# Two exponentials of a softmax head taken apart, and other places for the first loads of the tail

## Chip, cores and metric

One core of one Trainium2 chip. The metric is the device time of one execution in microseconds, median of several runs. Engines: TensorE (PE) with its weight loads (PEld), VectorE (DVE), ScalarE (ACT), GpSimd (POOL), and SyncE (SP), which only starts DMAs here. Each engine works through its own program in order; semaphores hold an instruction until what it reads, or what stands in the buffer that it writes, is done.

## The reference

One layer of a trunk with 1024 latent tokens, 128 context tokens and 256 cached ones, D_MODEL 1024, all float32:

```python
h = _rmsnorm(x, norm_g) * (1 + scale) + shift
u, v, g_a, c_q, c_kv, k_rope, g_b = _split_in(h @ w_in)
a_out = _chunk_mlp(u, v, w_s, b_s, g_v) * jax.nn.silu(g_a)
q = (_rmsnorm(c_q, q_norm_g) @ w_uq).reshape(B, L, MLA_HEADS, QK_NOPE + QK_ROPE)
...
s = jnp.concatenate(logits, axis=-1).astype(jnp.float32) * ATTN_SCALE
p = jax.nn.softmax(s, axis=-1).astype(v_all.dtype)
return jnp.einsum('bhqk,bkhv->bqhv', p, v_all)
...
y = jnp.concatenate([a_out, attn * jax.nn.silu(g_b)], axis=-1) @ w_o
return x + gate * y
```

Four heads attend from each block of 128 latent tokens to 1280 keys (1024 latent, 256 cached). The outputs of both halves go through w_o (1024 x 1024), are added to x under the gate, and get a last RMS norm.

## The kernel before

Precision is kept by splitting float32 values in two: a high part, which is a cast on ScalarE or POOL, and a low part, which DVE subtracts (lo_of, L112); a product is then three matmuls (high by high, high by low, low by high).

Up to 317 us the kernel normalises, projects and prepares queries and keys; the change leaves that alone. **Attention** follows, to about 505 us. There are 8 blocks t of 128 queries and 4 heads h; the head (t, h) is a step, two heads a pair. A period of PE's program holds the scores of one pair (score_steps, L1515 to L1519: one matmul group of 256 cached keys, two of 512 latent keys, for each head) and, merged between them by cost, the value stream of an earlier pair: five groups i = 0 to 4 of four 128x128 transposes (tr, L1562) into a PSUM ring of two buffers, and behind each the weighted sums with the compressed values (av, L1586 to L1588), then the copy os of the sums (L1596, ACT), their product with wuv (L1605) and the multiplication into mixB (L1607, DVE).

What sets the order on the other engines is `later(dt, fn)` (L167): the step is put into the program when PE's planned time has gone dt microseconds past the call. So the numbers in those calls fix the row in which an operation stands on ACT, DVE and POOL; at run time nothing overtakes.

softmax() (L1464 to L1510) plans for each head: the maximum over latent scores (L1481) and cached ones (L1484) and the shift nb (L1486 and L1487, or L1489) on DVE; exps (L1495), two ScalarE instructions, first 256 columns, then 1024, into e; divide: sum and reciprocal rs (L1499, L1500, DVE) and the multiplication of all 1280 columns (L1501, POOL). For each transposed group ACT casts the high part ph (L1566) and DVE subtracts the low part pl (L112); the subtraction frees the PSUM buffer for the group after next.

Beside the attention of blocks 1 to 5 run the units: weight sums T1 to T4 of quarters of w_o (t_unit, L1874), two a head pair, with subtractions on POOL (L809), casts thi on ACT (L1885), low parts into traw on DVE (L112), and stores to tdram by SP (L1881). From block 6 on pieces of w_o are split instead (spare_hi on POOL L115, spare_lo on DVE L112; the tiles area, ringB, ringC, kch, krh).

From 505 to 531 us the last two pairs' value streams run with early output products. The **output projection** (531 to 608 us) is a product by blocks with fewer multiplications; its left blocks (ring areas, made from mixA and mixB by casts L2152 and copies L2150 with lo_of) meet the sums T1 to T4 from tdram (t_pieces, L1919, DMAs issued by POOL; three matmuls at L1923 to L1925). A list planner (Plan, L45) orders its steps by cost, priority and due time; fetch (L2046) plans its loads one behind the other. The buffers of its pool ep lie over those of the attention pool, so a load can start only when the last reader of what lay there is done: `t1` (all of T1) lay over four tiles, two of them pieces of w_o, gate0 (loaded at L2053 by SP, read first at L2197) over the exponentials of head (7, 1) and the high part of the last transposed group.

Of the kernel before, what the change touches and what calls it, by code (L numbers as in the profile page):

```python
# [9 lines left out]
F32 = mybir.dt.float32  # L10
F32R = mybir.dt.float32r
BF16 = mybir.dt.bfloat16
I32 = mybir.dt.int32
AF = mybir.ActivationFunctionType
ALU = mybir.AluOpType
# [3 lines left out]
P = 128  # L19
NT = 9  # L20
NS = 8
# [73 lines left out]
def tile_hymba_step(ctx: ExitStack, tc: tile.TileContext, I, O):  # L95
    nc = tc.nc
    V, S, G, T = nc.vector, nc.scalar, nc.gpsimd, nc.tensor

    def opened(name, bufs=1, space=None, side=None):
        kw = dict(name=name, bufs=bufs, reuse_waits="tile")  # L100
        if space is not None:
            kw["space"] = space
        if side is not None:
            kw["side"] = side
        cm = tc.tile_pool(**kw)
        return cm, cm.__enter__()
# [60 lines left out]
    def later(dt, fn):  # L167
        waiting.append((now[0] + dt, fn))
        waiting.sort(key=lambda w: w[0])
# [17 lines left out]
    def step(cost, fn):  # L187

        catch_up(now[0])
        for f in list(fill):  # L190
            if f[0] in made and made_at[f[0]] <= now[0]:
                fill.remove(f)
                run(f[1:])
        run((cost, fn))
# [58 lines left out]
    tdram = gd.tile([4, P, 4, 2, 512], F32R, tag="tdram", name="tdram")  # L253
    scl = pc.tile([P, NT], F32, tag="scl", name="scl")
# [541 lines left out]
    def sums(n, k):  # L796
        c = 3072 * n + 768 * k
        return wide(c, GW), wide(c + GW, GW)

    T2, T3 = ([sums(n, k) for k in range(4)] for n in range(2))  # L800
    T4 = {k: sums(2, k) for k in range(2)}
    T1 = [(hh[k, 1], hl[k, 1]) for k in range(4)]
    t1 = {}
# [594 lines left out]
    if True:  # L1398
# [24 lines left out]
        c_kv, kv = opened("kv", side="left")  # L1423
# [4 lines left out]
        vh = kv.tile([P, 11, P], F32R, tag="vh", name="vh")  # L1428
        vl = kv.tile([P, 11, P], F32R, tag="vl", name="vl")
# [37 lines left out]
    units, traw, unit_of, paced = [], {}, [], [0]  # L1467
# [3 lines left out]
    def softmax(t, h, lat_, con_):  # L1471

        m = sm.tile([P, 2], F32, tag="m", name=f"m{t}{h}", bufs=3)
        nb = sm.tile([P, 1], F32, tag="nb", name=f"nb{t}{h}", bufs=3)
        su = sm.tile([P, 2], F32, tag="su", name=f"su{t}{h}", bufs=3)
        rs = sm.tile([P, 1], F32, tag="rs", name=f"rs{t}{h}", bufs=3)
        e = ap_.tile([P, 1280], F32, tag="e", name=f"e{t}{h}", bufs=6)
        es[t, h] = e

        def start():  # L1480
            V.tensor_reduce(m[:, 0:1], lat_, axis=AX.X, op=ALU.max)  # L1481

        def shift():
            V.tensor_reduce(m[:, 1:2], con_, axis=AX.X, op=ALU.max)  # L1484
            if units or t < 2 or (t, h) == (NS - 1, 3):
                V.tensor_reduce(nb, m, axis=AX.X, op=ALU.max)  # L1486
                V.tensor_scalar(nb, nb, nscl[:, t : t + 1], None, op0=ALU.mult)  # L1487
            else:
                V.scalar_tensor_tensor(nb, m[:, 0:1], m[:, 1:2], nscl[:, t : t + 1], op0=ALU.max, op1=ALU.mult)  # L1489
            later(0.6, exps)  # L1490
            later(1.3, lambda: spare_lo(1))

        def exps():
            for i, (src, sl) in enumerate(((con_, slice(1024, 1280)), (lat_, slice(0, 1024)))):
                S.activation(e[:, sl], src, AF.Exp, bias=nb, scale=scl[:, t : t + 1], accum_out=su[:, i : i + 1])  # L1495
            later(2.5 if t == 0 or (t, h) < (1, 2) else 1.9, divide)

        def divide():
            V.tensor_tensor(rs, su[:, 0:1], su[:, 1:2], op=ALU.add)  # L1499
            V.reciprocal(rs, rs)  # L1500
            G.tensor_scalar(e, e, rs, 0.0, op0=ALU.mult, op1=ALU.add)  # L1501
            made.add(("e", t, h))
            spare_hi(1 if his and his[0] in heavy else 2)
            spare_lo(2)
            if units and units[0][0] in traw:
                n_ = 1
                paced[0] += 1
                for i in range(n_):
                    unit_of[0](*units.pop(0), 2.2 * i)

        return start, shift
# [121 lines left out]
    def spare_hi(n):  # L1633
        for _ in range(min(n, len(his))):
            his.pop(0)()

    def spare_lo(n):
        for _ in range(min(n, len(los))):
            los.pop(0)()
# [148 lines left out]
    with tc.manual_schedule(engines=engines):  # L1788
# [77 lines left out]
        th, tl, his_ = {}, {}, {}  # L1866
# [46 lines left out]
        def t_pieces(m, k, hold, wide=512):  # L1913

            rows = hold.rearrange("p (a c) -> p a c", c=wide)[:, :, wide - 512 :]
            n = rows.shape[1] // 2
            for i in range(n):
                th[m, k + i], tl[m, k + i] = rows[:, 2 * i], rows[:, 2 * i + 1]
            G.dma_start(rows, tdram[m - 1, :, k : k + n].rearrange("p k s c -> p (k s) c"))  # L1919
# [37 lines left out]
        first = [s_ for i in range(LEAD) for s_ in score_steps(*heads[i])]  # L1957
# [61 lines left out]
    c_ep, ep = opened("ep", side="right")  # L2019
# [2 lines left out]
    spare_hi(len(his))  # L2022
    while los:
        spare_lo(1)
    t1 = ep.tile([P, 4096], F32R, tag="t1", name="t1")
    t4 = [ep.tile([P, 2048], F32R, tag="t4", name="t4"), *(kv.tile([P, 1024], F32R, tag=n, name=f"{n}t") for n in ("vh", "vl"))]
    fg = ep.tile([P, 1024], F32, tag="fg", name="fg")
    gate, ssq = {}, {}
    plan = Plan()
    plan.free.update(T=0.0, V=0.5, S=0.5, G=0.0, D=0.0)  # L2030
# [15 lines left out]
    def fetch(key, fn, deps=(), cost=1.35, lag=1.8):  # L2046
        last_ = [fetched[0]] if fetched[0] else []
        step(key, "D", cost, fn, [*deps, *last_], 0, lag=lag)
        fetched[0] = "|" + key

    def load_gate():
        gate[0] = ep.tile([P, 1024], F32, name="gate0", tag="gate0")
        nc.sync.dma_start(gate[0], gdram[0:1, :].broadcast_to([P, 1024]))  # L2053

    own = {}
# [1 line left out]
    def load_own(i, dma):  # L2057
        t_ = own[i] = ep.tile([P, 1024], F32, tag="xr", name=f"own{i}", bufs=4)
        dma(t_[:, 0:512], gdram[1:2, 512 * i : 512 * i + 512].broadcast_to([P, 512]))
        dma(t_[:, 512:1024], I["x"][8][:, 512 * i : 512 * i + 512])  # L2060

    fetch("gate0", load_gate, lag=4.5)
    for k in (0, 2):
        fetch(f"T1{k}", lambda k=k: t_pieces(1, k, t1[:, 1024 * k : 1024 * k + 2048]), cost=2.7)
    for k, piece in ((0, t4[0]), (2, t4[1]), (3, t4[2])):
        fetch(f"T4{k}", lambda k=k, piece=piece: t_pieces(4, k, piece), cost=1.35 if k else 2.7)
    fetch("own1", lambda: load_own(1, nc.scalar.dma_start))
    for t in (0, 1):
        fetch(f"x{t}", lambda t=t: load_xr(t))
# [71 lines left out]
    for q in range(3, len(queue)):  # L2141
        n, name, _ = queue[q]
# [96 lines left out]
            for t in PAIRS[nx]:  # L2239
                fetch(f"x{t}", lambda t=t: load_xr(t), {2: [], 3: ["a81"]}.get(t, [f"y{t - 4}"]))  # L2240

    landed = dict(T1=("T10", "T12"), T4=("T40", "T42", "T43"))

    def products():
        for q in range(1, 28):
# [174 lines left out]
```

## Time and profile before

| what | us |
|---|---|
| median of 3 runs | 617.89 (617.23 to 619.18) |
| the profiled execution | 617.24 |
| its span, first to last instruction | 615.5 |
| PE busy | 599.4 |
| DVE busy | 425.4 |
| ACT busy | 328.9 |
| POOL busy | 207.4 |
| mean granted clock of TensorE | 0.993 |

Busy time is that of one profiled execution. A row of the timeline gives start, duration, engine, line, operation, the tile written and those read, shapes, and in brackets how long the engine had been idle before it and which instruction's end it waited for. Where a helper records the operation (L112, L115, L809), the tile names tell which use it is. Ends of matmuls are modelled; starts are measured. Numbers of heads and blocks don't show in the names of the timeline.

### The profile page before, as it was taken

To read this page: it belongs to the slowest core of one execution; us is meant where nothing else is said; L and a number is where in the kernel's file an instruction comes from. 1 tells how busy PE (TensorE), PEld (TensorE's weight loads), DVE (VectorE), ACT (ScalarE), POOL (GpSimd) and SP (SyncE) were. 2 spreads that over 40 slices of the span, in tenths; PEclk is the share of its full clock that TensorE was granted. 3 is DMA by queue.
4 is the path that set the end of the run, shared out by engine and by line. 5 is a ranking of instruction groups with operands and counts; after the bars stand their busy time and mean duration, and the time that the engine had idled before them with its cause. 6 is when DMAs were issued, how large, how long until landed. Compare 5 with 4: busy or idle time off the path is not lost.

```text
span 615.5 us, 10221 instructions
## 1 busy us (share of the span) xinstructions
PE 599.4 (97%) x3671; PEld 541.4 (88%) x3671; DVE 425.4 (69%) x936; ACT 328.9 (53%) x765; POOL 207.4 (34%) x247
## 2 busy tenths in 40 slices
PE   8999999999999999999999999999999999999995
PEld 7678889999989999999998898888889988888885
DVE  4694458897756368476678667767678866478885
ACT  6556764345433245455567566565655553457543
POOL 2461112000000000443263344545344446259833
PEclk9999999999999999999999999999999999999998
DMA  8992010100351133100001043343241028761443
GB/s 314 393 381 82 1 34 2 35 0 6 133 207 70 68 96 131 40 1 1 1 27 51 1 129 129 121 135 123 87 135 71 1 70 286 281 254 40 148 147 145
DMA packets 30771, 67.33 MB, mean 109 GB/s; under 512 B 3312, under 2 KB 17408, under 8 KB 29568
## 3 DMA queue, kind: packets, MB, share of 16 engines
q1 hardware_dynamic: 27792, 55.93, 26.0%
q0 software_dynamic: 2064, 8.39, 3.9%
q10 hardware_dynamic: 864, 2.36, 1.1%
q8 instruction: 29, 0.48, 0.3%
q14 instruction: 22, 0.18, 0.1%
HBM read 53.45 MB, written 13.21 MB: 108 GB/s over the span
## 4 chain that ended last, share of the span: by engine, by line
PE 70%; DVE 16%; ACT 8%; issue 4%; DMA 1%; SPq 0%; ACTq 0%; DVEq 0%
PE p L954 10%; PE tp L752 8%; DVE pl L112 6%; PE tp L976 5%; ACT e L1495 5%; DVE m L1481 4%; PE zacc L1390 2%; PE zacc L1389 2%; PE zacc L1391 2%; PE S L1923 2%; PE S L1924 2%; PE S L1925 2%; ACT ph L1566 2%; DVE m L1484 2%; PE A L1924 1%
## 5 line engine op out<-in xcount | busy, mean ns | idle before, releaser
L1495 ACT ACTIVATE e<-s,nb,scl 128x256 f32<-128x256 f32 x64 | 56.1, 881 | 55.3 <-DVE nb L1487 39.7
L1501 POOL TENSOR_SCALAR e<-e,rs 128x1280 f32<-128x1280 f32 x32 | 47.3, 1478 | 104.3 <-ACT ph L1566 52.8
L112 DVE TENSOR_TENSOR pl<-pT,ph 128x512 fp32r<-128x512 f32 x81 | 55.4, 686 | 30.5 <-ACT ph L1566 29.0
L1237 POOL TENSOR_TENSOR kr<-z,rope 128x64 f32<-128x64 f32 x8 | 2.6, 324 | 172.3 <-ACT z L1246 172.3
L1566 ACT CAST ph<-pT 128x512 fp32r<-128x512 f32 x80 | 46.3, 587 | 25.8 <-PE pT L1562 24.5
L1562 PE MATMUL pT<-ident,e 128*128 128x128 f32 x320 | 48.6, 275 | 4.7 <-DVE pl L112 3.9
L752 PE MATMUL tp<-area,w 128*128 128x384 f32 x288 | 52.7, 339 | 0.0
L752 PEld LDWEIGHTS tp<-area,w 128*128 128x128 f32 x288 | 50.6, 188 | 0.4
L1586 PE MATMUL o<-ph,vh 128*128 128x256 f32 x160 | 47.7, 298 | 0.0
L1562 PEld LDWEIGHTS pT<-ident,e 128*128 128x128 f32 x320 | 37.0, 140 | 10.0 <-DVE pl L112 5.0
L1587 PE MATMUL o<-pl,vh 128*128 128x256 f32 x160 | 45.0, 281 | 0.0
L1588 PE MATMUL o<-ph,vl 128*128 128x256 f32 x160 | 45.0, 281 | 0.0
L1481 DVE TENSOR_REDUCE m<-s 128x1 f32<-128x1024 f32 x32 | 38.9, 1216 | 2.6 <-PE s L1519 2.5
L1515 PE MATMUL s<-kch,area 128*128 128x512 f32 (+2 forms) x100 | 39.2, 392 | 0.0
L1516 PE MATMUL s<-kcl,area 128*128 128x512 f32 (+2 forms) x100 | 35.3, 353 | 0.0
L1518 PE MATMUL s<-krh,area 128*128 128x512 f32 (+2 forms) x100 | 35.3, 353 | 0.0
L1517 PE MATMUL s<-kch,area 128*128 128x512 f32 (+2 forms) x100 | 35.2, 352 | 0.0
L1519 PE MATMUL s<-krl,area 128*128 128x512 f32 (+2 forms) x100 | 35.2, 352 | 0.0
L976 PE MATMUL tp<-area,w 128*128 128x384 f32 x192 | 35.0, 337 | 0.0
L976 PEld LDWEIGHTS tp<-area,w 128*128 128x128 f32 x192 | 33.6, 188 | 0.4 <-issue 0.4
L1586 PEld LDWEIGHTS o<-ph,vh 128*128 128x128 f32 x160 | 30.2, 189 | 1.4
L1587 PEld LDWEIGHTS o<-pl,vh 128*128 128x128 f32 x160 | 30.2, 189 | 1.4
(667 smaller groups left out, 1723.4 us busy)
## 6 DMA issues: line engine op xcount, KB each, us to landing
ada<-in_ada_ss SPq DMA_DIRECT2D x16, 512.0 KB, 8.1
w2r<-in_w_t SPq DMA_DIRECT2D x12, 512.0 KB, 4.4
x<-in_x SPq DMA_DIRECT2D x9, 512.0 KB, 7.4
adag<-in_ada_g SPq DMA_DIRECT2D x4, 1024.0 KB, 4.9
traw<-in_w_o SPq DMA_DIRECT2D x16, 256.0 KB, 3.2
tdram<-thi SPq DMA_DIRECT2D x32, 128.0 KB, 1.8
tdram<-traw SPq DMA_DIRECT2D x32, 128.0 KB, 1.8
wor<-in_w_o SPq DMA_DIRECT2D x8, 512.0 KB, 3.8
```

The costliest lines, as they stand in the source:

```text
L112: V.tensor_tensor(lo, src, f32(hi), op=ALU.subtract)
L752: T.matmul(tps[i, g][:, :GW], w_[i][:, k, :], x_[k, g], start=k == 0 and j == 0, stop=k == NK - 1 and j == 2)
L954: T.matmul(banks[key], a_, b_, start=k == 0 and m == 0, stop=k == 3 and m == len(passes) - 1)
L976: T.matmul(tps[c, 2][:, :GW], w_[c][:, k, :], x_[k, 2], start=k == 0 and m == 0, stop=k == NK - 1 and m == 2)
L1481: V.tensor_reduce(m[:, 0:1], lat_, axis=AX.X, op=ALU.max)
L1495: S.activation(e[:, sl], src, AF.Exp, bias=nb, scale=scl[:, t : t + 1], accum_out=su[:, i : i + 1])
L1501: G.tensor_scalar(e, e, rs, 0.0, op0=ALU.mult, op1=ALU.add)
L1562: T.transpose(ps[:, w : w + P], es[t, h][:, c * P : (c + 1) * P], ident)
L1566: later(0.5, lambda: S.copy(ph[:, :w], ps[:, :w]))
L1586: T.matmul(o, vh[:, kt, :], ph[:, sl], start=c == 0, stop=False)
L1587: T.matmul(o, vh[:, kt, :], pl[:, sl], start=False, stop=False)
L1588: T.matmul(o, vl[:, kt, :], ph[:, sl], start=False, stop=c == n - 1)
```

## The change

Three things. (1) The two exponentials of a head are two planned steps. For heads planned while units are left, and for block 1, they come 1.2 and 2.3 us after the shift and the division 3.9; before, both came at 0.6 and the division 2.5 or 3.1 after the shift. Other heads keep theirs. (2) Of the last head's division, DVE does columns 0 to 511 and POOL the other 768. (3) T1 is held in four tiles instead of one: t1a (rows 0 and 1), t1c (row 2), t1h and t1l (high and low part of row 3), loaded by four DMAs instead of two, and gate0 is placed ahead of some of them, so that all ep tiles have other addresses. The planner's rule that products with T1 wait for its landing is empty now (the semaphores still hold them).

```diff
-            later(0.6, exps)
+            apart = bool(units) or t == 1
+            later(1.2 if apart else 0.6, lambda: exp(0))
+            later(2.3 if apart else 0.6, lambda: exp(1))
+            later(3.9 if apart else 3.1 if t == 0 else 2.5, divide)
             later(1.3, lambda: spare_lo(1))
 
-        def exps():
-            for i, (src, sl) in enumerate(((con_, slice(1024, 1280)), (lat_, slice(0, 1024)))):
-                S.activation(e[:, sl], src, AF.Exp, bias=nb, scale=scl[:, t : t + 1], accum_out=su[:, i : i + 1])
-            later(2.5 if t == 0 or (t, h) < (1, 2) else 1.9, divide)
+        def exp(i):
+            src, sl = ((con_, slice(1024, 1280)), (lat_, slice(0, 1024)))[i]
+            S.activation(e[:, sl], src, AF.Exp, bias=nb, scale=scl[:, t : t + 1], accum_out=su[:, i : i + 1])
 
         def divide():
             V.tensor_tensor(rs, su[:, 0:1], su[:, 1:2], op=ALU.add)
             V.reciprocal(rs, rs)
-            G.tensor_scalar(e, e, rs, 0.0, op0=ALU.mult, op1=ALU.add)
+            first = 512 if (t, h) == (NS - 1, 3) else 0
+            if first:
+                V.tensor_scalar(e[:, :first], e[:, :first], rs, None, op0=ALU.mult)
+            G.tensor_scalar(e[:, first:], e[:, first:], rs, 0.0, op0=ALU.mult, op1=ALU.add)
...
-    t1 = ep.tile([P, 4096], F32R, tag="t1", name="t1")
-    t4 = [ep.tile([P, 2048], F32R, tag="t4", name="t4"), *(kv.tile([P, 1024], F32R, tag=n, name=f"{n}t") for n in ("vh", "vl"))]
-    fg = ep.tile([P, 1024], F32, tag="fg", name="fg")
+    def place(name, w, dt=F32R):
+        return ep.tile([P, w], dt, tag=name, name=name)
+
+    t4 = [place("t4", 2048)]
+    t1h, t1a = place("t1h", 512), place("t1a", 2048)
+    gate0, fg = place("gate0", 1024, F32), place("fg", 1024, F32)
+    t1c, t1l = place("t1c", 1024), place("t1l", 512)
+    t4 += [kv.tile([P, 1024], F32R, tag=n, name=f"{n}t") for n in ("vh", "vl")]
+    th[1, 3], tl[1, 3] = t1h, t1l
...
-    for k in (0, 2):
-        fetch(f"T1{k}", lambda k=k: t_pieces(1, k, t1[:, 1024 * k : 1024 * k + 2048]), cost=2.7)
-    for k, piece in ((0, t4[0]), (2, t4[1]), (3, t4[2])):
-        fetch(f"T4{k}", lambda k=k, piece=piece: t_pieces(4, k, piece), cost=1.35 if k else 2.7)
+    fetch("T10", lambda: t_pieces(1, 0, t1a), cost=2.7)
+    fetch("T12", lambda: t_pieces(1, 2, t1c))
+    fetch("T1h", lambda: G.dma_start(t1h, tdram[0, :, 3, 0, :]), cost=0.7)
+    fetch("T40", lambda: t_pieces(4, 0, t4[0]), cost=2.7)
+    fetch("T1l", lambda: G.dma_start(t1l, tdram[0, :, 3, 1, :]), cost=0.7)
+    for k in (2, 3):
+        fetch(f"T4{k}", lambda k=k: t_pieces(4, k, t4[k - 1]))
...
-    landed = dict(T1=("T10", "T12"), T4=("T40", "T42", "T43"))
+    landed = dict(T1=(), T4=("T40", "T42", "T43"))
```

What that moves in the engines' programs. First ScalarE, one period in block 4 (the e rows are the exponentials of two heads, ph_3 and ph_4 the casts of one pair's last groups, ph_0 to ph_2 those of the next pair, thi a weight sum's high part). Before:

```order
L1495 ACTIVATE e_4582,su_4580<-s_3422,nb_4579,scl 128x256
L1495 ACTIVATE e_4582,su_4580<-s_4529,nb_4579,scl 128x1024
L1566 CAST ph_3_4645<-pT_3_4640 128x512
L1566 CAST ph_4_4677<-pT_4_4672 128x512
L1885 CAST thi_4698<-traw_4430 128x512
L1495 ACTIVATE e_4657,su_4655<-s_3422,nb_4654,scl 128x256
L1495 ACTIVATE e_4657,su_4655<-s_4629,nb_4654,scl 128x1024
L1566 CAST ph_0_4712<-pT_0_4707 128x512
L1885 CAST thi_4724<-traw_4430 128x512
L1566 CAST ph_1_4733<-pT_1_4728 128x512
L1596 COPY os_4766<-o_4618 128x256
```

The same stretch of the change (lines of the code are 3 to 5 higher):

```order
L1498 ACTIVATE e_4574,su_4572<-s_3422,nb_4571,scl 128x256
L1571 CAST ph_3_4644<-pT_3_4639 128x512
L1498 ACTIVATE e_4574,su_4572<-s_4529,nb_4571,scl 128x1024
L1571 CAST ph_4_4677<-pT_4_4672 128x512
L1890 CAST thi_4708<-traw_4447 128x512
L1571 CAST ph_0_4706<-pT_0_4701 128x512
L1498 ACTIVATE e_4656,su_4654<-s_3422,nb_4653,scl 128x256
L1571 CAST ph_1_4725<-pT_1_4720 128x512
L1498 ACTIVATE e_4656,su_4654<-s_4629,nb_4653,scl 128x1024
L1890 CAST thi_4743<-traw_4447 128x512
L1601 COPY os_4760<-o_4618 128x256
```

Each second exponential has moved behind one cast, and the second head's first exponential has moved behind the cast ph_0, which stood behind both of its exponentials before.

Second DVE, where the last head is divided (rs is the sum and reciprocal, pl the low parts, ringC and kcl low parts of projection operands). Before:

```order
L1499 TENSOR_TENSOR rs_5736<-su_5735 128x1
L1500 RECIPROCAL rs_5736<-rs_5736 128x1
L112 TENSOR_TENSOR pl_0_5804<-pT_0_5798,ph_0_5803 128x512
L112 TENSOR_TENSOR pl_1_5818<-pT_1_5812,ph_1_5817 128x512
L112 TENSOR_TENSOR pl_2_5846<-pT_2_5840,ph_2_5845 128x512
L112 TENSOR_TENSOR ringC<-mixB,ringC 128x512
L1607 TENSOR_TENSOR mixB<-mixB,at_5867 128x2x128
L112 TENSOR_TENSOR pl_3_5883<-pT_3_5877,ph_3_5882 128x512
```

With the change:

```order
L1501 TENSOR_TENSOR rs_5734<-su_5733 128x1
L1502 RECIPROCAL rs_5734<-rs_5734 128x1
L1505 TENSOR_SCALAR e_5735<-e_5735,rs_5734 128x512
L112 TENSOR_TENSOR pl_0_5804<-pT_0_5798,ph_0_5803 128x512
L112 TENSOR_TENSOR pl_1_5818<-pT_1_5812,ph_1_5817 128x512
L112 TENSOR_TENSOR pl_2_5845<-pT_2_5839,ph_2_5844 128x512
L1612 TENSOR_TENSOR mixB<-mixB,at_5865 128x2x128
L112 TENSOR_TENSOR pl_3_5881<-pT_3_5875,ph_3_5880 128x512
```

An operation on half a thousand columns of e stands between the reciprocal and pl_0; the low part of ringC has left the stretch (it stands further on, behind the last pair's pl_3).

Third POOL, behind the last division, up to the loads for the output projection (ringC is part of a left block, area, kch and krh hold pieces of w_o, t_6057 T1, t_6058 part of T4). Before:

```order
L115 TENSOR_SCALAR ringC<-mixB 128x512
L115 TENSOR_SCALAR kch_5784<-wor_5786 128x512
L1919 DMA area_118<-tdram 128x4x512
L1919 DMA area_119<-tdram 128x4x512
L115 TENSOR_SCALAR kch_5784<-wor_5786 128x512
L115 TENSOR_SCALAR krh_5788<-wor_5790 128x512 x2
L115 TENSOR_SCALAR area_120<-wor_5792 128x512 x2
L1919 DMA t_6057<-tdram 128x2048 x2
L1919 DMA t_6058<-tdram 128x2048
```

With the change:

```order
L115 TENSOR_SCALAR kch_5784<-wor_5786 128x512
L1924 DMA area_118<-tdram 128x4x512
L1924 DMA area_119<-tdram 128x4x512
L115 TENSOR_SCALAR kch_5784<-wor_5786 128x512
L115 TENSOR_SCALAR krh_5788<-wor_5790 128x512 x2
L115 TENSOR_SCALAR area_120<-wor_5792 128x512 x2
L115 TENSOR_SCALAR ringC<-mixB 128x512
L1924 DMA t1a<-tdram 128x2048
L1924 DMA t1c<-tdram 128x1024
L2076 DMA t1h<-tdram 128x512
L1924 DMA t_6058<-tdram 128x2048
L2078 DMA t1l<-tdram 128x512
```

The copy into ringC has moved from ahead of kch to behind area_120's two copies; the loads of T1 (two of 128x2048 in t_6057 before) are t1a, t1c, t1h and t1l, the last behind the load of t_6058.

More of the change, by code (lines that the diff above doesn't have):

```diff
@@ L2051, in load_gate @@
     def load_gate():
-        gate[0] = ep.tile([P, 1024], F32, name="gate0", tag="gate0")
+        gate[0] = gate0
         nc.sync.dma_start(gate[0], gdram[0:1, :].broadcast_to([P, 1024]))
```

## The prediction

> **What bounds the kernel now.** I read the page first, for the engine that is nearly always busy, then the busy time by windows for where it is not, then the timeline at the gaps, row by row. The page:
>
> ```profile
> PE 599.4 (97%) x3671; PEld 541.4 (88%) x3671; DVE 425.4 (69%) x936; ACT 328.9 (53%) x765; POOL 207.4 (34%) x247
> ```
>
> TensorE (PE) is busy for 599.4 of 615.5 us, so a change that takes no matmul away can gain only what PE loses waiting. The change touches nothing ahead of the attention (317 us onward), so only the waits behind that count. Of six windows in a row, which run from the third transpose group of one period to that of the next (a period computes the scores of two heads and transposes two earlier ones), the first, the third and the last are shown; columns are length, then busy time of PE, its weight loads, DVE, ACT and POOL, then granted clock, DMA share and GB/s:
>
> ```profile
> 370.40:383.02 12.62, 12.21 (x85) 11.10 (x85) 9.02 (x21) 7.61 (x17) 5.83 (x6) 1.00 0.38 125
> ...
> 396.00:408.62 12.62, 12.19 (x84) 11.10 (x84) 9.02 (x21) 7.61 (x17) 5.84 (x6) 1.00 0.39 126
> ...
> 433.88:446.32 12.44, 12.19 (x84) 11.10 (x85) 8.87 (x20) 7.60 (x17) 5.82 (x6) 1.00 0.26 86
> ```
>
> The periods lose 0.25 to 0.43 us each by this count, at full clock, while no other engine is busy for more than 9.02 us of 12.62. So PE waits for a chain, not for an engine that is full. Here is that chain (start, duration, engine and line, operation, idle time before it and who ended it):
>
> ```profile
> 396.04 0.16 DVE L1500 RECIPROCAL rs<-rs 128x1 f32<-128x1 f32 x1
> ...
> 396.12 0.69 DVE L112 TENSOR_TENSOR traw<-traw,thi 128x512 fp32r<-128x512 f32 x1
> ...
> 396.40 1.63 POOL L1501 TENSOR_SCALAR e<-e,rs 128x1280 f32<-128x1280 f32 x1 [3.80 <-ACT ph L1566]
> ...
> 401.56 0.29 PE L1588 MATMUL o<-ph,vl 128*128 128x256 f32 x1
> ...
> 401.69 0.60 PE L1562 MATMUL pT<-ident,e 128*128 128x128 f32 x4
> ...
> 404.58 0.60 PE L1562 MATMUL pT<-ident,e 128*128 128x128 f32 x4
> ...
> 405.53 0.56 ACT L1495 ACTIVATE e<-s,nb,scl 128x256 f32<-128x256 f32 x1 [2.04 <-DVE nb L1487]
> 406.08 1.20 ACT L1495 ACTIVATE e<-s,nb,scl 128x1024 f32<-128x1024 f32 x1
> 407.26 0.58 ACT L1566 CAST ph<-pT 128x512 fp32r<-128x512 f32 x1
> 407.88 0.69 DVE L112 TENSOR_TENSOR pl<-pT,ph 128x512 fp32r<-128x512 f32 x1 [1.60 <-ACT ph L1566]
> 407.92 0.28 PE L1588 MATMUL o<-ph,vl 128*128 128x256 f32 x1
> 408.62 0.66 PE L1562 MATMUL pT<-ident,e 128*128 128x128 f32 x4 [0.43 <-DVE rs L1499]
> 410.42 0.39 PE L1515 MATMUL s<-kch,area 128*128 128x512 f32 x1
> ```
>
> The transposes of 404.58 end at 405.18, and ScalarE could cast them (0.58) at once. But the two exponentials stand ahead of that cast, one behind the other, until 407.28. So the cast ends at 407.84, DVE's subtraction at 408.57, and only then is the PSUM buffer free that the transposes of 408.62 write. (The row names DVE's rs, which starts as the subtraction's buffer comes free; the late one is the subtraction.)
>
> How much a wait costs I take from starts, since the ends of matmuls are modelled: behind the same L1588 matmul transposes start after 0.13 us where nothing holds them (401.56, 401.69), and after 0.70 here (407.92, 408.62), which is 0.57 lost; the held group itself then takes 0.66 and not 0.60. So 0.63 us are lost, and 12.62 - 0.63 = 11.99 us is the period without the wait.
>
> **The attention periods.** The six windows reach from 370.40 to 446.32, which is 75.92 us; six of 11.99 are 71.94, so 3.98 us are lost inside them. At both edges stands one more wait of the kind:
>
> ```profile
> 370.04 0.28 PE L1588 MATMUL o<-ph,vl 128*128 128x256 f32 x1
> 370.40 0.66 PE L1562 MATMUL pT<-ident,e 128*128 128x128 f32 x4
> ...
> 449.28 0.60 PE L1605 MATMUL at<-os,wuv 128*128 128x128 f32 x4
> 450.20 0.63 PE L1562 MATMUL pT<-ident,e 128*128 128x128 f32 x4 [0.32 <-DVE pl L112]
> ```
>
> 370.40 came 0.36 behind its matmul and not 0.13, with 0.06 of the longer group 0.3 us; 450.20 came 0.92 behind the L1605 group, which occupies PE for about 0.4, so 0.5 lost. Together 3.98 + 0.3 + 0.5 = 4.8 us.
>
> With a cast between the two exponentials, the wait chain is first exponential (0.56), cast (0.58), subtraction (0.69). Laid out from one third group (0) to the next (11.99) with the durations above: in the first half the exponential starts at 3.3, the cast at 3.96, the second exponential at 4.6 to 5.8. In the second half the shift is ready at 8.4, the cast of the next pair's first transposes runs 9.17 to 9.76, the first exponential behind it, and the subtraction ends at 10.5, which is what the third transposes wait for at 11.99: 1.5 us to spare where 0.63 was missing. The second exponential now ends at 12.15 from the period's start and not 11.3. The output copies, the reciprocals and POOL's divisions move back by 1 to 2 us too; the division's reader comes over 5 us behind it, so nothing waits. In the last period that has weight sums, the head behind it keeps its exponentials together; by the same layout its subtraction ends at 12.14, and 0.2 us stays. Term: **-4.6 us** (bounds: 0, if another wait takes each place, and -4.8).
>
> The first value pair has a larger wait of the same kind:
>
> ```profile
> 337.89 0.60 PE L1562 MATMUL pT<-ident,e 128*128 128x128 f32 x4
> ...
> 340.07 1.20 ACT L1495 ACTIVATE e<-s,nb,scl 128x1024 f32<-128x1024 f32 x1
> ...
> 341.12 0.40 PE L1519 MATMUL s<-krl,area 128*128 128x512 f32 x1
> 342.71 0.63 PE L1562 MATMUL pT<-ident,e 128*128 128x128 f32 x4 [1.19 <-DVE pl L112]
> ```
>
> Transposed by 338.49, cast only behind the exponential that ends at 341.27. PE starts 1.59 behind its last matmul, of which 0.23 is that matmul: 1.36 lost. With the cast first, the subtraction ends at about 340.4 (behind DVE's shift and reciprocal), ahead of PE's 341.35. Term: **-1.4 us** (0 to -1.4).
>
> **The last head.** DVE's reciprocal, its subtraction and PE's wait there, and an operation of the added kind:
>
> ```profile
> 506.12 0.16 DVE L1500 RECIPROCAL rs<-rs 128x1 f32<-128x1 f32 x1
> 506.40 1.29 DVE L112 TENSOR_TENSOR pl<-pT,ph 128x512 fp32r<-128x512 f32 x2
> ...
> 506.34 0.39 PE L1954 MATMUL w<-area,ml 128*128 128x512 f32 x1
> 507.14 0.66 PE L1562 MATMUL pT<-ident,e 128*128 128x128 f32 x4 [0.41 <-DVE pl L112]
> ```
>
> ```profile
> L2302 DVE TENSOR_SCALAR own<-own,rlast 128x512 f32<-128x512 f32 x1 | 0.5, 489 | 0.0
> ```
>
> PE already waits here for the first of those subtractions (0.80 behind its matmul and not 0.23, so 0.57). The added piece of 128x512, 0.49 by the row, goes between the reciprocal and that subtraction, and DVE's low parts for the weights come one division later, some 0.1 more. POOL gets its division's end half a microsecond sooner, for which nobody on PE waits. Term: **+0.5 us** (+0.3 to +0.8).
>
> On the two engines at once the trace has one sign. POOL's divisions (shortest, median and longest of 32, in ns):
>
> ```profile
> L1501 POOL TENSOR_SCALAR e<-e,rs x32: 1332/1348/1898, 321.4 to 506.5; 128x1280 f32<-128x1280 f32 x32
> ```
>
> The one at 396.40 ran beside DVE's L112 of 396.12, which reads two SBUF operands until 396.81, and took 1.63 us and not 1.35. After a reciprocal DVE's next operation starts first (396.12 against 396.40), so if either piece of the last division waits, it is POOL's, and nobody on PE's path needs that sooner than now; the term stays.
>
> **The tail.** Three things move (the rows with KB are DMA issues, with the median us from issue to landing):
>
> ```profile
> 525.13 0.40 PE L1925 MATMUL f<-area,ringC 128*128 128x512 f32 x1
> 525.36 0.60 PE L1562 MATMUL pT<-ident,e 128*128 128x128 f32 x4
> ```
>
> ```profile
> 524.77 0.69 DVE L112 TENSOR_TENSOR pl<-pT,ph 128x512 fp32r<-128x512 f32 x1 [0.90 <-ACT ph L1566]
> ```
>
> POOL's copy for ringC now stands behind two copies that wait for a piece of w_o, and DVE's low part of ringC behind the subtraction of 524.77: it ends near 525.46 + 0.68 = 526.1. The matmul at 525.13 reads it; four matmuls of 0.23 are put ahead of that one, so it would start at 526.05. **+0.1 us** (0 to +0.3).
>
> ```profile
> 528.85 0.33 SPq L2053 DMA_DIRECT2D gate<-gdram x1
> ```
>
> ```profile
> t<-tdram POOLq DMA_DIRECT2D x3, 1024.0 KB, 8.2
> ...
> vlt<-tdram POOLq DMA_DIRECT2D x1, 512.0 KB, 13.0
> ```
>
> ```profile
> 537.26 0.69 DVE L2197 TENSOR_TENSOR mixB<-f,gate 128x512 f32<-128x512 f32 x1 [2.94 <-DMA gate<-gdram]
> ```
>
> ```profile
> 537.09 0.39 PE L1925 MATMUL S<-area,ringB 128*128 128x512 f32 x1
> 538.05 0.47 PE L1923 MATMUL S<-t,ringC 128*128 128x512 f32 x1 [0.57 <-ACT ringB L2152]
> ```
>
> The gate's load is issued at 528.85, behind the last weighted sum, because its buffer lies over that sum's operand; it lands 8.4 us later, DVE waits 2.94 us for it, and the product at 538.05 waits for the bank that DVE empties: 0.96 behind the matmul at 537.09, against 0.23, and with 0.08 of its longer time 0.8 us. (The row names a cast of ScalarE that ends in the same tenth of a microsecond; this product does not read what it writes.) The gate's new place lies over buffers last read by the transposes of 525.36, so the load goes at about 526 to 527 and lands 2 us sooner; the bank is free in time. Term: **-0.8 us** (0 to -0.8). The first weight sum's own pieces start sooner too, all but the last of 256 KB, which now lies over that late operand. It is needed about 1.6 us into the products (539.7). From its issue near 529.9 on it has 9.8 us, where the loads of 1024 KB landed 8.2 us from issue; I put its landing at 534 to 538.
>
> **The sum.** -4.6 - 1.4 + 0.5 + 0.1 - 0.8 = -6.2 us. The profiled execution took 617.24 us (span 615.5 and 1.7 around it), so it would take 611.0; the median of the runs is 0.65 us above that execution, so **611.7 us**.
>
> **Rivals.**
> - *The wait only changes hands in the periods.* If DVE, on which maximum, reciprocal and subtraction are queued in a new order, delivers the subtraction as late as now, the -4.6 is lost and the others stay: 617.89 - 1.6 = 616.3. Against it: DVE has 3.6 idle us in each period, 1.60 of them directly ahead of that subtraction. Half of it lost gives 614. Together 0.12.
> - *The late piece.* If the 256 KB behind the last weighted sum land as late as the row of vlt (13.0 us after its issue near 529.9, so 542.9), PE stands for 3.2 us: 614.9. Against it: that load had three of 1024 KB and one more ahead of it, all issued in the 3 us before; here most of the bytes ahead were issued from 523.6 on. 0.06.
> - *POOL's piece first.* If DVE's piece waits until POOL's 768 columns are done, 1.33 x 768/1280 = 0.8 us, the subtraction behind it is 0.8 later still, and the wait of 507.14 grows by 1.3 and not 0.5: 611.7 + 0.8 = 612.5. For it speaks that 1.63 at 396.40, where two such operations met; against it that DVE was the first there. 0.07. [...]
> - *Slower.* The second exponential holds a score bank longer. In the second half of a period it now ends 0.87 later, while the next score matmul into such a bank (410.42, 1.80 behind the third group) comes 0.63 sooner: of 410.42 - 407.28 = 3.1 us 1.6 remain. From 1.6 us of further delay on, each period loses what is beyond; with 2.6 us it is 1 us at each of eight pairs, 8 us against the 6.2: 619.7. ScalarE would have to be far behind its rows. 0.04.
>
> **How the numbers follow.** The forecast as worked out has 0.71, the rivals 0.12, 0.06, 0.07 and 0.04. The bounds of the terms alone, without the rivals, give 611.2 to about 613.5 (the last head at +0.8, ringC at +0.3, the gate at 0, one more half microsecond in the periods); runs of one kernel scatter by some 0.6 around the median. The range is **610.3 to 615.0**, which takes in that scatter, the late piece, POOL's piece first and the half-lost periods. This kernel's measurement can tell 0.3%, 1.85 us, from no change: faster below 616.04. Of the first rival the full loss, half of its 0.12, counts as same, the rest and the other cases as faster. Faster 0.90, same 0.06, slower 0.04.
>
> **What would show it.** Right: periods of 12.0 us between third groups up to 446, PE starting within 0.15 of its matmul there; no idle time before the fourth group of the first pair; the wait of 507.14 grown to about 1.1; no wait of DVE for the gate long enough to hold the first S product. Wrong: the transposes still released by DVE pl with over 0.3 us in each period; idle time of PE ahead of an s matmul, released by ACT e (the bank); a wait of an S product for a DMA of t1l.

## The result, and the profile after

The changed kernel takes 614.07 us (median of 6 runs, 613.09 to 614.5) where the kernel before, run beside it, takes 618.07 (6 runs, 617.23 to 619.41): a ratio of 0.993, 95% interval 0.9915 to 0.9945, or 4.0 us less (3.4 to 5.3). The forecast was 611.7, in a range of 610.3 to 615.0: the direction and the range held, the size was 6.2 against 4.0.

The two profiled executions differ by less, 615.5 against 612.7 us of span, and the place where they differ must be known before anything else is read. The first transposes of the attention start at 332.37 us before and at 334.28 after, and nothing ahead of them was changed. In the twelve profiles of this study they start between 332.17 and 334.28; that much the beginning scatters from execution to execution. So the traces are compared from the first transposes on, up to the start of the last store: that store is 2.73 us earlier, and 2.73 + 1.91 = 4.64 us are gained between the two. Step by step (starts of the same transpose group of PE, and the shift after minus before):

| place | before | after | shift | change of the shift |
|---|---|---|---|---|
| first transposes | 332.37 | 334.28 | +1.91 | |
| behind the first pair's wait | 342.71 | 343.25 | +0.54 | -1.37 |
| last of the third groups | 446.32 | 443.34 | -2.98 | -3.52 |
| fourth group of that period | 450.20 | 447.93 | -2.27 | +0.71 |
| last pairs | 504.04 | 501.50 | -2.54 | -0.27 |
| last head's wait | 507.14 | 505.07 | -2.07 | +0.47 |
| start of the last store | 611.91 | 609.18 | -2.73 | -0.66 |

The -0.27 between the fourth group and the last pairs had no term in the forecast. Of it, 0.18 lies at the transposes of 498.81 before: there PE had 0.17 us of idle time behind a subtraction of DVE, and has none now. What moved that subtraction forward was not tested.

The busy time by windows of the kernel after, again from third group to third group (length; PE, weight loads, DVE, ACT, POOL; clock):

```profile
370.78:382.87 12.09, 12.09 (x87) 11.15 (x85) 9.06 (x21) 7.73 (x18) 5.83 (x6) 1.00 0.40 131
...
431.24:443.34 12.10, 12.10 (x87) 11.16 (x86) 7.57 (x19) 8.17 (x19) 5.84 (x6) 1.00 0.23 77
```

PE is busy for the whole of each window: the wait of the period is gone, as forecast. But a period without it lasts 12.09 us and not 11.99. Here is the chain, to be laid beside that of 404 to 409 before (timeline, ACT, DVE and PE rows):

```profile
391.51 0.60 PE L1567 MATMUL pT<-ident,e 128*128 128x128 f32 x4
...
392.20 0.58 ACT L1571 CAST ph<-pT 128x512 fp32r<-128x512 f32 x1 [1.80 <-PE pT L1567]
392.68 0.57 ACT L1498 ACTIVATE e<-s,nb,scl 128x256 f32<-128x256 f32 x1
...
393.35 0.59 ACT L1571 CAST ph<-pT 128x512 fp32r<-128x512 f32 x1
393.83 1.21 ACT L1498 ACTIVATE e<-s,nb,scl 128x1024 f32<-128x1024 f32 x1
...
392.81 0.69 DVE L112 TENSOR_TENSOR pl<-pT,ph 128x512 fp32r<-128x512 f32 x1 [1.41 <-ACT ph L1571]
...
394.84 0.28 PE L1593 MATMUL o<-ph,vl 128*128 128x256 f32 x1
394.96 0.60 PE L1567 MATMUL pT<-ident,e 128*128 128x128 f32 x4
```

The cast starts 0.09 us behind the end of its transposes (392.11) where it waited 2.1 us before; the subtraction ends at 393.50, 1.46 us ahead of the transposes that need its buffer, and these follow the matmul of 394.84 after 0.12.

The 0.10 us by which a period is longer than forecast have a place too: 0.08 of them stand 1.1 us behind the third group. ACT and PE there, after, then PE before:

```profile
395.53 0.38 ACT L1601 COPY os<-o 128x256 f32<-128x256 f32 x1
...
395.99 0.36 PE L1591 MATMUL o<-ph,vh 128*128 128x256 f32 x1
396.19 0.28 PE L1592 MATMUL o<-pl,vh 128*128 128x256 f32 x1
```

```profile
409.71 0.28 PE L1586 MATMUL o<-ph,vh 128*128 128x256 f32 x1
409.83 0.28 PE L1587 MATMUL o<-pl,vh 128*128 128x256 f32 x1
```

The two matmuls start 0.20 us apart and not 0.12, in each of the six periods. The copy os of the sums before them now stands behind the second exponential and a cast: it ends 0.95 us behind the start of the third group, where it ended 0.50 behind it. The weight load of the matmul of 395.99 starts at 395.97, just behind the copy's end at 395.91; before, it started with the matmul ahead of it (both 409.59). Behind the third group of 443.34 the copy ends after 0.57 us, and there the step is 0.12 again. No run moved the copy alone.

One wait has grown, and it is one that the forecast had counted as gone. DVE and PE at the fourth group of the last period with weight sums, after:

```profile
444.78 1.21 DVE L1481 TENSOR_REDUCE m<-s 128x1 f32<-128x1024 f32 x1
445.91 0.68 DVE L112 TENSOR_TENSOR traw<-traw,thi 128x512 fp32r<-128x512 f32 x1
446.51 0.41 DVE L1484 TENSOR_REDUCE m<-s 128x1 f32<-128x256 f32 x1
446.96 0.22 DVE L1489 SCALAR_TENSOR_TENSOR nb<-m,nscl 128x1 f32<-128x1 f32 x1
447.10 0.68 DVE L112 TENSOR_TENSOR pl<-pT,ph 128x512 fp32r<-128x512 f32 x1
...
446.24 0.60 PE L1610 MATMUL at<-os,wuv 128*128 128x128 f32 x4
447.93 0.63 PE L1567 MATMUL pT<-ident,e 128*128 128x128 f32 x4 [1.08 <-DVE pl L112]
```

DVE at the same place before:

```profile
447.65 1.22 DVE L1481 TENSOR_REDUCE m<-s 128x1 f32<-128x1024 f32 x1
448.79 0.42 DVE L1484 TENSOR_REDUCE m<-s 128x1 f32<-128x256 f32 x1
449.24 0.22 DVE L1489 SCALAR_TENSOR_TENSOR nb<-m,nscl 128x1 f32<-128x1 f32 x1
449.37 0.68 DVE L112 TENSOR_TENSOR pl<-pT,ph 128x512 fp32r<-128x512 f32 x1
```

The subtraction (449.37 before, 447.10 after) has no idle time ahead of it in either kernel: DVE works through its queue, and a weight sum's low part (traw, 0.68 us) now stands in that queue too. PE comes 1.69 behind the L1610 group where it came 0.92 behind it before.

The last head and the gate, DVE, POOL and PE:

```profile
503.73 0.16 DVE L1502 RECIPROCAL rs<-rs 128x1 f32<-128x1 f32 x1
503.93 0.49 DVE L1505 TENSOR_SCALAR e<-e,rs 128x512 f32<-128x512 f32 x1
504.33 1.28 DVE L112 TENSOR_TENSOR pl<-pT,ph 128x512 fp32r<-128x512 f32 x2
...
504.10 1.09 POOL L1506 TENSOR_SCALAR e<-e,rs 128x768 f32<-128x768 f32 x1 [3.17 <-ACT ph L1571]
...
505.07 0.66 PE L1567 MATMUL pT<-ident,e 128*128 128x128 f32 x4 [0.86 <-DVE pl L112]
...
533.40 0.69 DVE L2211 TENSOR_TENSOR mixB<-f,gate 128x512 f32<-128x512 f32 x1 [1.02 <-DMA gate<-gdram]
...
535.15 0.39 PE L1930 MATMUL S<-area,ringB 128*128 128x512 f32 x1
535.38 0.40 PE L1928 MATMUL S<-t1a,ringC 128*128 128x512 f32 x1
```

DVE's piece takes 0.49 but delays the subtraction by 0.32: from the reciprocal's start to the subtraction's it is 0.60 us and was 0.28 (506.12 to 506.40), for the subtraction had 0.12 us of idle time ahead of it before, and the rows now overlap by 0.09. The gate still lands late for DVE, by 1.02 and not 2.94 us, but the bank is free in time: the first S product on the new tile follows after 0.23.

### The profile page after: what moved, and what is told of

The parts are those of the page before. It is cut to its first block, busy times and chain, and to the rows that moved or that the text cites. A ratio compares the mean times of both kernels' runs of the same rounds, so it can differ in the third digit from the quotient of the medians.

```text
span 612.7 us, 10225 instructions
## 1 busy us (share of the span) xinstructions
PE 599.2 (98%) x3671; PEld 542.2 (88%) x3671; DVE 426.1 (70%) x937; ACT 330.2 (54%) x765; POOL 208.4 (34%) x249
## 4 chain that ended last, share of the span: by engine, by line
PE 92%; DMA 2%; DVE 2%; ACT 1%; issue 1%; SPq 0%; ACTq 0%; DVEq 0%
PE p L954 9%; PE tp L752 8%; PE pT L1567 6%; PE tp L976 6%; PE s L1520 3%; PE o L1591 3%; PE s L1523 3%; PE s L1521 3%; PE s L1522 3%; PE s L1524 3%; PE o L1593 3%; PE o L1592 3%; PE zacc L1390 2%; PE zacc L1389 2%; PE zacc L1391 2%; PE S L1928 2%
## 5 line engine op out<-in xcount | busy, mean ns | idle before, releaser
L1506 POOL TENSOR_SCALAR e<-e,rs 128x1280 f32<-128x1280 f32 (+1 forms) x32 | 46.9, 1466 | 101.4 <-ACT ph L1571 41.5
```

## The experiments

Ten runs, in three groups on one chip each. For each stands the change of the shift between the same groups as in the table, so that the scatter of the beginning plays no part, beside the times.

**One part alone: the exponentials.**

```diff
-            later(0.6, exps)
+            apart = bool(units) or t == 1
+            later(1.2 if apart else 0.6, lambda: exp(0))
+            later(2.3 if apart else 0.6, lambda: exp(1))
+            later(3.9 if apart else 3.1 if t == 0 else 2.5, divide)
...
```

> The kernel before with the first part of the change alone: the two exponentials and the division of a head placed as in the change; nothing else. Theory A (the transposes waited because a cast stood behind both exponentials in ScalarE's order): the wait at the first pair's fourth step goes (1.4 us), the third groups of the six periods no longer wait (0.5 to 0.6 each, 3.5 us), and the wait at the fourth group of the last period with weight sums grows by 0.7, as in the profile of the change; together -4.4 us from 367 groups on, with the waits of the last head (0.6) and of the first S product on t (0.7) as before: about 613.8 us. Theory B (the gain came from the tail's placement or the divided division): less than 1 us faster, 617 or more.

Measured: 615.97 us against 617.69, ratio 0.9972 (0.9955 to 0.999), 1.7 us faster and not 4. The attention did what theory A says, within 0.2 us (-1.37 at the first pair, -3.68 in the periods, +0.75 at the fourth group). The tail gave much of it back. DVE, then PE, of this run, and PE's window behind it:

```profile
536.54 0.69 DVE L2199 TENSOR_TENSOR mixB<-f,gate 128x512 f32<-128x512 f32 x1 [4.43 <-DMA gate<-gdram]
```

```profile
534.88 0.39 PE L1927 MATMUL S<-area,ringB 128*128 128x512 f32 x1
537.34 0.47 PE L1925 MATMUL S<-t,ringC 128*128 128x512 f32 x1 [2.07 <-issue]
...
538.52 0.63 PE L1926 MATMUL S<-t,ringC 128*128 128x512 f32 x1
538.95 0.63 PE L1927 MATMUL S<-t,ringC 128*128 128x512 f32 x1
```

```profile
537.30:541.50 4.20, 4.17 (x11) 3.29 (x12) 1.73 (x3) 0.00 (x0) 0.00 (x0) 0.60 0.74 274
```

DVE now waits 4.43 us for the gate where it waited 2.94. In this order four projection matmuls of 0.23 stand ahead of the last weighted sums and no longer behind them, so the end of those sums, which lets the gate's load go, comes that much nearer to the place where the gate is needed; and the load, issued at 527.56, lands 9.0 us later where it took 8.4 before. PE stands for 2.07 us, and then its granted clock is 0.60: matmuls come every 0.43 us and not every 0.23.

**One part alone: the places of the loads** (the third part of the diff).

> The kernel before with the third part alone: T1 in four tiles and loads, gate0 over buffers that end earlier. Theory A: only the first S product on t gains; its wait of 0.7 us at 538 goes, because the gate lands before DVE needs it or about 1 us behind; 0.7 to 0.8 us faster, 617.3, and the attention periods stay at 12.6 us. Theory B (smaller DMAs behind one another cost as much as they give): no change, 618.0.

Measured: 617.26 against 617.69, ratio 0.999 (0.9978 to 1.0003): by time alone not told from no change. By the trace, 0.03 us less from the first to the last transposes and 0.70 less behind them; the attention is untouched and the tail's wait is gone. Theory A, and its size, from the trace.

**One part alone: the divided division** (the second part of the diff).

> The kernel before with the second part alone: the last head's division on DVE (512 columns) and POOL (768). Theory A: DVE's piece of 0.49 us stands ahead of the subtraction that the transposes at 507 wait for; that wait grows from 0.57 to 1.0; 0.45 us slower, 618.5. POOL's piece takes about 1.1 us, not 0.8, since it starts while DVE's runs. Theory B (POOL's earlier end helps what follows): 0.3 us faster or more.

Measured: 618.48 against 617.69, ratio 1.0015 (1.0001 to 1.0028). The wait of the last head grows by 0.33. POOL's piece, in this run too:

```profile
506.63 1.10 POOL L1504 TENSOR_SCALAR e<-e,rs 128x768 f32<-128x768 f32 x1 [3.29 <-ACT ph L1569]
```

DVE's piece ran from 506.47 to 506.96. From there to POOL's end at 507.73 it is 0.77 us, which is what 768 of 1280 columns of 1.33 us make (0.80); POOL's row of 1.10 is 0.30 longer than that, and DVE's ran beside it for 0.33 (506.63 to 506.96). DVE, which started first, lost nothing (0.49, as the lone row before). What makes POOL's row longer no run here shows.

**Is it the order on ScalarE, or the later divisions?**

```diff
-            later(0.6, exps)
+            apart = bool(units) or t == 1
+            later(0.6, lambda: exp(0))
+            later(0.6, lambda: exp(1))
+            later(3.9 if apart else 3.1 if t == 0 else 2.5, divide)
```

> The kernel before with the two exponentials together as before, but the division planned 3.9 us behind the shift where the change does so; the reciprocals and the weight sums that the division sets off stand as late as in the change. Theory A (ScalarE's order of cast and exponentials): the third groups still wait, and longer, because the cast of a weight sum's high part now stands between the second exponential and the cast that they need: about 1.1 us each and not 0.57, some 3 us slower, 621; the first pair's wait of 1.4 us stays. Theory B (the later reciprocals and weight sums free DVE for the subtraction): periods near 12.1 us, about 614.5.

Measured: 632.58 us, ratio 1.0234 (1.0209 to 1.0259), 15 us slower. Theory B is out. Theory A had the sign and the chain, not the size. ACT, DVE and PE of one period:

```profile
425.56 1.20 ACT L1498 ACTIVATE e<-s,nb,scl 128x1024 f32<-128x1024 f32 x1
...
426.74 0.61 ACT L1887 CAST thi<-traw 128x512 fp32r<-128x512 f32 x1
427.25 1.07 ACT L1568 CAST ph<-pT 128x512 fp32r<-128x512 f32 x2
...
427.87 0.69 DVE L112 TENSOR_TENSOR pl<-pT,ph 128x512 fp32r<-128x512 f32 x1 [2.90 <-ACT ph L1568]
...
428.62 0.55 PE L1564 MATMUL pT<-ident,e 128*128 128x128 f32 x3 [1.34 <-DVE pl L112]
```

Third groups come 0.9 us later per period than before, which the expectation had at 0.5, and a second wait, 0.4 us at each fourth group, was not in it at all. In the profiled execution, the quickest of the four, 11.4 us are lost up to the last head's transposes and 1.8 behind them, where PE waits 1.87 us at the first S product on t (550.93), as in the first run. So the later division is no gain by itself: it sets off the weight sums, and with the exponentials where they were these stand in the way. The converse, the exponentials apart and the division at its old place, was not run.

**The wait that grew: one DVE instruction moved in the changed kernel.**

```diff
-            for dt, fn, i in ((3.2, high, 0), (4.6, low, 0), (5.0, high, 1), (6.4, low, 1)):
+            for dt, fn, i in ((3.2, high, 0), (4.6, low, 0), (5.0, high, 1), (8.0 if u == 7 else 6.4, low, 1)):
```

> The changed kernel with one DVE instruction moved: the last weight sum's second low part (0.68 us), which stands between the two maxima ahead of the subtraction that the fourth group of the last period with weight sums waits for, goes behind that subtraction. Theory A (the wait there grew by just that instruction): it falls from 1.4 to 0.6 us or so, 0.7 us faster than the changed kernel, 613.3. Theory B (the transposes there wait for ScalarE's cast or for another engine): no change, 614.0.

Measured: 612.48 us against 617.68 of the kernel before, ratio 0.9918 (0.99 to 0.9936). The step at the fourth group is +0.12 and not +0.71, so 0.59 of the expected 0.7. DVE and PE there:

```profile
443.10 1.22 DVE L1481 TENSOR_REDUCE m<-s 128x1 f32<-128x1024 f32 x1
444.23 0.42 DVE L1484 TENSOR_REDUCE m<-s 128x1 f32<-128x256 f32 x1
444.68 0.22 DVE L1489 SCALAR_TENSOR_TENSOR nb<-m,nscl 128x1 f32<-128x1 f32 x1
444.81 0.68 DVE L112 TENSOR_TENSOR pl<-pT,ph 128x512 fp32r<-128x512 f32 x1
...
445.65 0.52 PE L1567 MATMUL pT<-ident,e 128*128 128x128 f32 x3 [0.49 <-DVE pl L112]
```

The rest of that wait is the two maxima and the shift ahead of the subtraction, as before the change. From the first transposes to the last store this run takes 5.13 us less than before, the changed kernel 4.64: the fastest kernel of the study by its trace and by its median, though the intervals of the two ratios (0.99 to 0.9936, 0.9915 to 0.9945) overlap.

**The division undivided in the changed kernel.**

```diff
-            first = 512 if (t, h) == (NS - 1, 3) else 0
...
+            G.tensor_scalar(e, e, rs, 0.0, op0=ALU.mult, op1=ALU.add)
```

> The changed kernel with the last head's division on POOL alone again. Theory A: the wait of the transposes at 505 falls from 1.0 to 0.6 us, 0.45 us faster than the changed kernel, 613.6; POOL's division takes 1.35 us and its later steps have slack. Theory B (POOL's half microsecond is needed for the left blocks of the projection): the same as the changed kernel or slower, 614.0 to 614.5.

Measured: 613.48 us, ratio 0.9929 (0.991 to 0.9948), not to be told from the changed kernel. The wait of the last head falls by 0.33, and theory B takes it back: two matmuls on a piece of w_o start 0.1 us late each, two on ringC 0.1 and 0.2, as POOL's copies and DVE's low parts come later. In the periods and behind 530 nothing differs.

**Both waits.** The undivided division, the low part moved, and the subtraction of the fourth group ahead of the second maximum and the shift:

```diff
-            later(1.15, low)
+            later(0.55 if (t, pr, i) == (4, 1, 2) else 1.15, low)
...
```

> The changed kernel without the split division, with the low part moved as in the run before last, and with the subtraction ahead of the cached keys' maximum and the shift at that one place. Theory A: the wait at the fourth group falls from 1.4 to at most 0.2 us (1.2 gained), the last head's from 1.0 to 0.6 (0.45 gained): 612.4, faster than both kernels. Theory B: the shift, 0.7 us later there, delays that head's exponentials and a later wait takes the place: 613.5.

Measured: 612.94 us, ratio 0.9921 (0.9906 to 0.9937). Theory B: the step at the fourth group is -0.54, so that wait is gone, and 0.33 us each are lost at the two steps behind the next pair's groups. DVE:

```profile
445.03 0.68 DVE L112 TENSOR_TENSOR pl<-pT,ph 128x512 fp32r<-128x512 f32 x1
445.63 0.42 DVE L1484 TENSOR_REDUCE m<-s 128x1 f32<-128x256 f32 x1
```

The shifts come later, the next heads' two exponentials (not apart there) with them, and the cast and subtraction behind those; that is the first of the two steps. At the second the subtraction has no idle time ahead of it: DVE's queue is late by then. From the first transposes to the last store it is 5.04 us less than before, no better than the run with only the low part moved.

**The slower rival of the prediction, made on purpose.**

```diff
-            later(2.3 if apart else 0.6, lambda: exp(1))
-            later(3.9 if apart else 3.1 if t == 0 else 2.5, divide)
+            later(5.2 if apart else 0.6, lambda: exp(1))
+            later(6.8 if apart else 3.1 if t == 0 else 2.5, divide)
```

> The changed kernel with the second exponential planned 5.2 us behind the shift and the division 6.8, so that in the second half of a period it stands behind the third group's cast too. This is the slower rival of the prediction, with its price. By the layout of the prediction the second exponential then ends about 2.7 us behind the third group, and the score matmul that needs its bank stands at 1.8: 0.9 us lost at each of the eight pairs with weight sums, +7 us on the changed kernel, 621; idle time of PE ahead of an s matmul, released by the exponential. If the bank has more room than the layout gives it: 614, no idle time there.

Measured: 630.01 us, ratio 1.0193 (1.0176 to 1.021): 12.3 us slower than before, 16 slower than the change. PE's waits from 327 us on, and two of them:

```profile
PE s L1520 <- ACT e L1498: 13.7, 16, 1.1
```

```profile
412.43 0.50 PE L1520 MATMUL s<-kch,area 128*128 128x512 f32 x1 [1.14 <-ACT e L1498]
419.67 0.50 PE L1520 MATMUL s<-kch,area 128*128 128x512 f32 x1 [0.63 <-ACT e L1498]
```

The bank is where the layout has it, and the wait at the second head is 0.63 idle (0.87 in starts) where 0.9 was expected. But there are 16 of them: the first head of each pair waits too, and longer (1.41 in starts), which the expectation had left out.

**Which of the moved loads matters?** The exponentials alone, and the gate's tile alone in another place:

```diff
+    gate0 = ep.tile([P, 1024], F32, tag="gate0", name="gate0")
     t4 = [ep.tile([P, 2048], F32R, tag="t4", name="t4"), *(kv.tile([P, 1024], F32R, tag=n, name=f"{n}t") for n in ("vh", "vl"))]
...
-        gate[0] = ep.tile([P, 1024], F32, name="gate0", tag="gate0")
+        gate[0] = gate0
```

> The exponentials alone (the kernel of the first run), and one tile of the tail placed elsewhere: gate0 is taken from its pool ahead of T4's first tile, so that it lies over a piece of w_o that is done by 521, not over the operand of the last weighted sum. T1 stays one tile with its two loads. Theory A (the gate's late landing alone made the wait of 2.1 us at the first S product on t, and the slow clock behind it): the load goes 2 to 3 us sooner, that wait and the slow matmuls are gone (1.4 + 1.6 us against the first run's profile), 613.5, and T1's pieces are no part of the gain. Theory B (T1's first load is late too): a wait of over 0.5 us stays there, on a DMA of t.

Measured: 613.75 us against 618.12, ratio 0.9928 (0.9908 to 0.9948). The DVE row of the gate has no idle time any more, and PE follows on with a matmul of 0.40 us, where the slow ones of the first run took 0.63:

```profile
530.36 0.68 DVE L2200 TENSOR_TENSOR mixB<-f,gate 128x512 f32<-128x512 f32 x1
...
533.44 0.40 PE L1925 MATMUL S<-t,ringC 128*128 128x512 f32 x1
```

With T1 in one tile and two loads, no wait for a piece of t is left, so what the first S product gains is the gate's. Behind the last transposes this run is 0.30 us longer than the changed kernel with the undivided division; the difference lies in two waits for low parts of DVE (0.13 at 567.25, 0.17 at 578.46) and in no load. Whether the four pieces brought about the order without these waits was not tested; the profiles show no other gain of theirs.

**The slow clock again.**

> The kernel of the first run once more, for a second profile. If the idle time of 2.1 us ahead of the first S product on t is what brought the matmuls behind it down to half speed, they are slow again whenever that idle time is 2 us or more, and at full speed where it is clearly less; the attention's steps repeat within 0.05 us either way.

Measured: 616.35 us in one run. The idle time was longer this time, and the granted clock over the 4.2 us behind it 1.00:

```profile
537.16 0.47 PE L1925 MATMUL S<-t,ringC 128*128 128x512 f32 x1 [2.42 <-issue]
537.47 0.39 PE L1926 MATMUL S<-t,ringC 128*128 128x512 f32 x1
```

So the length of the idle time alone does not decide it: 0.60 behind 2.07 us, 1.00 behind 2.42 us, in two executions of the same kernel. What does decide it no run here shows.

## Why the prediction was right in direction and range, and too large

- **First pair, -1.4:** measured -1.37. Right, chain and size.
- **Third groups of the periods:** right in mechanism, too large by about 0.10 us a period. The forecast had 3.98 + 0.3 for them at 11.99 us a period; it was 3.52 at 12.09. The 0.57 of waiting and the 0.06 of the held group both went as counted. The step that failed is the sentence on the output copies: "the division's reader comes over 5 us behind it, so nothing waits". It looks at the division's reader only; the output copy, moved back with the exponential, ends at 0.95 us behind the third group, and the sums behind it start 0.08 late. The other 0.02 are spread.
- **The fourth group at 450.20, -0.5:** wrong, the largest miss: +0.71. The row named DVE pl, and the prediction took it as "one more wait of the kind". It was of another kind: the subtraction had no idle time before it, so it waited for DVE's own queue (two maxima and the shift) and not for a cast behind exponentials. And the later division moved a low part of 0.68 us into that queue, which nothing in the sum had looked for. Moving that instruction out again gave 0.59 back.
- **Last head, +0.5:** measured +0.47, the size in part by luck. The piece of 0.49 cost 0.33 (the changed kernel against the undivided, and the division alone, both 0.33), and the exponentials alone cost 0.14 here where the forecast had some 0.1. That POOL's earlier end is worth nothing was wrong for the changed kernel, where it saves 0.47 at 515 to 524; with the division alone it saves 0.03 there.
- **ringC, +0.1:** about +0.17. The four matmuls are moved ahead of it as said, the matmul on ringC (524.01) then starts 0.06 us late, and the transposes behind it 0.11.
- **Gate, -0.8:** -0.66 behind the last head with ringC's +0.17 in it. In the part alone the first S product gains 0.83, and 0.13 of that is lost again at a wait for a low part of DVE at 571. Right in size, for a reason that was only half seen: with the exponentials moved and the gate left in place, the tail would have lost 1.5 us more in waiting, and in one execution 1.5 more at a granted clock of 0.60. The terms were added as if they did not touch each other.
- **Together:** of the forecast's 6.2 us the traces show 4.64. The third groups are 0.8 short; the fourth group is 1.0 off, counting the 0.2 that the forecast let stay; the 0.27 without a term came on top. The 4.0 of the medians has an interval (3.4 to 5.3) that holds 4.64. That half of the first rival's loss gives 614, next to the measured 614.07, is chance: in the periods the wait did not change hands.
- **The late piece:** t1l was no wait (issued at 528.07, landed 7.4 us later, first read by the matmul of 537.72, without idle time); POOL's piece first did not happen (DVE's ran 0.49 from 503.93 on, POOL's 1.09 from 504.10 on); the bank was free (PE's waits from 327 us on are two, 1.9 us together, both for DVE pl).
- **The base:** the execution profiled before had one of the quickest beginnings (332.37), the one after the slowest (334.28). The ratio of the medians is not touched by it; the 2.73 between the two profiles' last stores is.

## What to carry to other kernels

A wait's releaser names the last link only. Before a group of waits is priced as one kind, look at the idle time ahead of the releaser itself: with idle time it waited for a chain, without it it stood in its own engine's queue; here reordering ScalarE took away the waits of the first kind, and the one of the second kind grew. And when steps are planned one from another, as the weight sums are from the division, follow every instruction that moves with them to where it now stands, and ask who reads or overwrites what it uses: here one of 0.68 us took back an eighth of the gain, and an output copy that came 0.5 us later cost 0.08 us in every period.

## What was not expected of the hardware

After 2.07 us without matmuls the granted clock was 0.60 over the next 4.2 us in one execution, and it was 1.00 after 2.42 us in another of the same kernel; what decides it stays open. And the beginning, the same program in all profiles, scatters by 2 us. A part of that is the pace of PE's first long run of matmuls. Before, the matmuls on vacc at 16.65 and 16.89 start 0.24 us apart; after, those at 17.79 and 18.22 start 0.43 apart. The granted clock from 16 to 18 us was 0.91 in the one and 0.50 in the other. It is not the only part: in the second profile of the exponentials alone the clock there was 1.00, and its first transposes still came at 333.59. A difference of 2 us between two single spans says nothing about a change that starts at 330 us.
